# The last two tiles of the out projections, the layer norm and the first two tiles of the next stage, by halves of the 512 tokens

## The chip, the cores and the metric

The kernel runs on one core of one Trainium2 chip. The time is the device time of one execution in microseconds. A core has five engines that run side by side, each through its own instructions in order: PE (matrix multiplication), DVE (vector), ACT (activations and copies), POOL (general vector work) and SP, which here only issues DMAs. They wait for each other by semaphores.

## The reference

Two blocks follow each other on a sequence of 512 tokens with 2048 features, all in float32. The first has two layers of one form:

```python
for l in range(DEPTH):                       # 2 layers
    u = x @ w_in[l]                          # 2048 -> all branches
    y_conv, y_mla, y_rwkv = ...              # convolution, attention, RWKV-7
    mix = jnp.concatenate([y_conv, y_mla, y_rwkv], axis=-1)      # 2048 features
    x = _layer_norm(DEEPNORM_ALPHA * x + mix @ w_out[l], ln_g[l], ln_b[l])
```

The second block begins with `h = rms_norm(x, ln_gain)` and `proj = h @ w_in_2` and goes on with differential attention, a state-space branch, gates, two projections and an output projection, to which x is added. A layer norm needs the mean and the variance over all 2048 features of a token, so nothing of the next stage's `x @ w_in` for a token can start before the whole out projection of that token is done.

## The kernel before

Activations lie transposed: features on the 128 partitions, tokens along the free axis. A vector of 2048 features is 16 tiles of 128 x 512. Float32 products are made of three passes: weights and activations are each split into a rounded high part (fp32r) and a low part, and `mm3` (lines 178 to 185) adds high x high, high x low and low x high, 48 matmuls for one output tile of 128 features. `load_w` brings a tile's weights in two pieces of 512 KB; ACT casts the high part (`wh`, three buffers) and DVE subtracts for the low part (`wl`, three buffers).

The instructions of each engine are put in order when the program is built, by a scheduler that reckons with its own times; on the chip each engine keeps that order. Around the change the order of work is this:

- `out_proj` (line 1100) makes 16 output tiles. Each gets the residual added on DVE (line 1146) and its square from ACT (line 1153). POOL adds tiles and squares up over the tiles (lines 1163, 1164); in the last layer DVE keeps three weighted sums more (lines 1166, 1168), since layer norm and the next block's RMS norm are folded into one step there. Between the tiles, the preparation of the state-space branch (`ssm_prep`) runs in pieces on DVE, ACT and POOL.
- While the last tile is on PE, small matmuls against unit vectors (line 1138) turn the running sums into per-token columns in PSUM (`ps_st`); the last tile's own share comes last (lines 1175, 1177).
- DVE works out mean and variance in columns of four numbers per partition (lines 1186 to 1196), POOL the power of -1/2 (line 1202), twice in the last layer. PE transposes the columns into rows (lines 376, 1238), ACT copies these to SBUF (lines 1239, 1241).
- For each of the 16 tiles a multiply (line 1250, five of them on POOL), a matmul of six rows for the shift (line 1252), a multiply-add that reads it from PSUM (line 1253) and the split into high and low part (lines 175 and 176, three low parts on POOL) make the next stage's x.
- The next stage begins with two output tiles at once (`inproj_group`, line 193): for each feature tile q, as soon as its x is there, six matmuls. The third output tile needs one of the two accumulators and so waits until a copy on ACT has freed it.

This happens twice: between the layers, and between the second layer and the second block. Between two boundaries PE works through tiles of `mm3` one behind the other.

## Time and profile before

| | us |
|---|---|
| median of 3 runs | 3318.41 |
| lowest, highest | 3317.36, 3320.7 |
| profiled execution | 3319.2 |
| its span, first to last instruction | 3317.5 |

| engine | busy us | share of the span | instructions |
|---|---|---|---|
| PE matmul | 3271.4 | 99% | 16291 |
| DVE | 1738.0 | 52% | 2783 |
| ACT | 1123.2 | 34% | 1842 |
| POOL | 706.9 | 21% | 925 |

Matmuls are pipelined: one of 512 columns is shown as busy for 0.39 us, but the next starts 0.23 us later. So a stretch in which PE is shown as busy all the time may still be one in which it runs below its rate: the starts say more than the busy time. Granted clock is the share of TensorE's full clock of 2.4 GHz; the lower of its two levels is 1.2 GHz.

### The profile page before, as it was taken

The numbers are of one execution on the slowest core, as the hardware profiler recorded it, in microseconds if no ns is written. First come the engines' busy times: TensorE is split into PE (matmuls) and PEld (weight loads), VectorE is DVE, ScalarE is ACT, GpSimd is POOL, SyncE is SP. The second block draws the span as 40 slices with busy tenths as digits, with TensorE's granted clock in tenths as the row PEclk, the third lists the DMA queues.
The fourth block names the chain that finished last, engine by engine and source line by source line (L and its number), as shares of the span: only waits on it lengthen the run. The fifth ranks groups of instructions, "written<-read, shape, count | busy, mean of one in ns | idle before, by whom it ended". The sixth has DMA issues, their size and how long they took to land. (4 is left out here: it accounts for less than half of the span.)

```text
span 3317.5 us, 42703 instructions
## 1 busy us (share of the span) xinstructions
PE 3271.4 (99%) x16291; PEld 2686.6 (81%) x16291; DVE 1738.0 (52%) x2783; ACT 1123.2 (34%) x1842; POOL 706.9 (21%) x925
## 2 busy tenths in 40 slices
PE   9999999999999999999999999999999999999999
PEld 7787888877878778888878688888888888888887
DVE  4536835655663459446567666555555533323432
ACT  4332223444333222224532234344444322222332
POOL 1234622012421036321123321111110000001011
PEclk9999999999999999999999899999999999999999
DMA  6455544435544554445255243333333633333543
GB/s 173 149 178 151 145 128 146 125 89 157 168 151 126 151 160 131 144 134 154 80 157 150 84 117 105 102 102 102 100 98 119 221 102 105 102 106 101 158 146 111
DMA packets 672832, 433.81 MB, mean 131 GB/s; under 512 B 91286, under 2 KB 615851, under 8 KB 672627
## 3 DMA queue, kind: packets, MB, share of 16 engines
q1 hardware_dynamic: 668754, 419.02, 42.5%
q0 software_dynamic: 3296, 11.01, 1.1%
q8 instruction: 128, 2.10, 0.3%
q10 hardware_dynamic: 576, 1.05, 0.1%
q14 instruction: 78, 0.63, 0.1%
HBM read 351.30 MB, written 79.69 MB: 130 GB/s over the span
## 5 line engine op out<-in xcount | busy, mean ns | idle before, releaser
L183 PE MATMUL acc<-xh,wh 128*128 128x512 f32 x3552 | 1394.1, 394 | 11.3 <-ACT c L778 5.0
L185 PE MATMUL acc<-xh,wl 128*128 128x512 f32 x3552 | 1398.4, 394 | 2.0 <-DVE wl L169 2.0
L184 PE MATMUL acc<-xl,wh 128*128 128x512 f32 x3552 | 1397.5, 394 | 2.6 <-DVE xl L176 2.3
L169 DVE TENSOR_TENSOR wl<-wr,wh 128x1024 fp32r<-128x1024 f32 (+1 forms) x508 | 662.4, 1304 | 873.5 <-ACT wh L168 850.3
L168 ACT CAST wh<-wr 128x1024 fp32r<-128x1024 f32 (+1 forms) x508 | 530.5, 1045 | 1468.4 <-PE acc L184 1204.0
L183 PEld LDWEIGHTS acc<-xh,wh 128*128 128x128 f32 x3552 | 669.3, 189 | 155.0 <-ACT c L778 6.1
L184 PEld LDWEIGHTS acc<-xl,wh 128*128 128x128 f32 x3552 | 669.1, 188 | 147.7 <-DVE xl L176 6.8
L185 PEld LDWEIGHTS acc<-xh,wl 128*128 128x128 f32 x3552 | 669.2, 188 | 140.5 <-DVE wl L169 2.9
L1836 POOL TENSOR_TENSOR b<-b,b 128x512 f32<-128x512 f32 x16 | 21.1, 1316 | 499.0 <-DVE b L1834 499.0
L396 POOL TENSOR_TENSOR rr_a<-rv_a,mhalf 128x8 f32<-128x8 f32 (+1 forms) x24 | 35.9, 1495 | 280.7 <-DVE rv_a L391 280.7
L1163 POOL TENSOR_TENSOR b<-b,b 128x512 f32<-128x512 f32 x28 | 49.6, 1772 | 181.4 <-DVE b L1146 174.8
L1834 DVE SCALAR_TENSOR_TENSOR b<-b,ps_b 128x512 f32<-128x512 f32 x32 | 22.0, 688 | 105.5 <-PE ps_b L185 105.5
L598 DVE TENSOR_TENSOR pk<-pk,pk 128x224 f32<-128x224 f32 (+59 forms) x126 | 69.9, 555 | 3.4
L599 DVE TENSOR_TENSOR pk<-pk,pk 128x224 f32<-128x224 f32 (+59 forms) x126 | 65.3, 518 | 3.5
L966 POOL TENSOR_TENSOR v<-v,c 128x512 f32<-128x512 f32 x16 | 20.6, 1288 | 185.0 <-ACT v L963 185.0
L562 DVE TENSOR_TENSOR pk<-ps_m,mrk 128x512 f32<-128x512 f32 x32 | 22.0, 689 | 68.9 <-PE ps_m L559 68.8
L825 ACT ACTIVATE a<-ps_a,nm_a,sp_a 128x128 f32<-128x128 f32 (+3 forms) x64 | 39.2, 615 | 44.1 <-DVE nm_a L822 40.4
L1854 POOL TENSOR_TENSOR b<-b,ln 128x512 f32<-128x512 f32 x16 | 20.7, 1293 | 151.6 <-DVE b L1853 126.1
L183 PE MATMUL acc<-n,wh 128*128 128x512 f32 x128 | 52.4, 409 | 0.1
L694 POOL COPY zw_pk<-zwh_pk 64x128 f32<-64x128 f32 x64 | 22.0, 343 | 139.8 <-ACT zwh_pk L687 137.0
L184 PE MATMUL acc<-n,wh 128*128 128x512 f32 x128 | 51.2, 400 | 0.0
L183 PE MATMUL ps_b<-ya,wh 128*128 128x512 f32 x128 | 50.7, 396 | 0.0
(519 smaller groups left out, 4017.2 us busy)
## 6 DMA issues: line engine op xcount, KB each, us to landing
wr<-in_w_in_dram SPq DMA_DIRECT2D x336, 512.0 KB
wr<-in_w_out_dram SPq DMA_DIRECT2D x96, 512.0 KB
pack<-pk SPq DMA_DIRECT2D x32, 576.0 KB
pk<-pack SPq DMA_DIRECT2D x24, 576.0 KB
b<-xd SPq DMA_DIRECT2D x48, 256.0 KB
c<-mix SPq DMA_DIRECT2D x32, 256.0 KB
xd<-b SPq DMA_DIRECT2D x32, 256.0 KB
wr<-in_w_proj_att_dram SPq DMA_DIRECT2D x16, 512.0 KB
```

Source lines behind the costliest of these rows:

```text
L168: nc.scalar.copy(hi[:, : m * n], raw[:, : m * n])
L169: nc.vector.tensor_tensor(out=lo[:, : m * n], in0=raw[:, : m * n], in1=hi.bitcast(F32)[:, : m * n], op=ALU.subtract)
L183: self.nc.tensor.matmul(out, lhsT=wh, rhs=xh, start=st, stop=False)
L184: self.nc.tensor.matmul(out, lhsT=wh, rhs=xl, start=False, stop=False)
L185: self.last = self.nc.tensor.matmul(out, lhsT=wl, rhs=xh, start=False, stop=sp)
L396: nc.gpsimd.tensor_tensor(out=r.rearrange(flat), in0=v.rearrange(flat), in1=k.mhalf[:, 0:n], op=ALU.pow)
L562: nc.vector.tensor_tensor(out=pk[:, i, O_G:].rearrange("p (h c t) -> p h c t", h=2, c=2), in0=ps[:, :, 0:256].rearrange("p h (c t) -> p h ...
L598: eng.tensor_tensor(out=t3, in0=X[:, 0:n, c - 1 : c].to_broadcast([P, n, w]), in1=q[:, q.shape[1] - w :].unsqueeze(1).to_broadcast([P, n, ...
L599: eng.tensor_tensor(out=X[:, 0:n, c:], in0=X[:, 0:n, c:], in1=t3, op=A)
L694: nc.gpsimd.tensor_copy(out=Wd[o, u, c].rearrange("p (h w) -> p h w", w=64), in_=Wh[o, u, 0:4:3, :])
L825: nc.scalar.activation(out=pr[:, 0:n], in_=ps[:, 0:n], func=AF.Exp, scale=scale, bias=nm, accum_out=sm)
L1163: nc.gpsimd.tensor_tensor(out=sums[0], in0=sums[0], in1=t, op=ALU.add)
```

## The change

- The last two of the 16 output tiles, 14 and 15, are made in halves of 256 tokens: both tiles for the first 256, then both for the second, with the weights of both kept. `load_w` gets a parameter `spare`: the second piece of tile 15's weights goes into two buffers of the `r4` kind, which are otherwise the preparation's.
- Tiles 14 and 15 are no longer added to the running sums. Their share of the columns comes by small matmuls, per half and tile.
- The columns, the powers, the transposes and the copies are made per half (`stats(h)`), each with two columns in place of four. The multiply now always reads ACT's copy of the row (`As`), no longer PSUM.
- Normalisation and split go in the order: tiles 0 to 7 of the first half, tiles 0 to 7 of the second, tiles 8 to 15 of the first, and of the second. `inproj_group` follows this order for the stages behind a layer norm. Each output row of x is written to memory in two DMAs.
- PSUM: three `b` and one `st` buffers become two and two.

```diff
-    def load_w(self, parts, kt, n, side=False):
+    def load_w(self, parts, kt, n, side=False, spare=None):
...
+                if spare and k0 + m == kt:
+                    hi, lo = (self.b4((P, WCH), F32R, spare) for _ in range(2))
+                else:
...
-        for q in range(KT):
-            for i, ps in enumerate(pss):
-                self.mm3(ps, sub(w[q : q + 1], slice(i * P, i * P + P)), x[q : q + 1], q == 0, q == KT - 1)
+        for q0 in range(0, KT, KT // 2):
+            for ts in HALVES if halves else (slice(0, S),):
+                for q in range(q0, q0 + KT // 2):
+                    for i, ps in enumerate(pss):
+                        self.mm3(ps[:, ts], sub(w[q : q + 1], slice(i * P, i * P + P)), sub(x[q : q + 1], ts),
+                                 q == 0 and ts.start == 0, q == KT - 1 and ts.stop == S)
...
-    with k.phase(f"p{l}o", {"b": 3, "r": 2, "st": 1}, b=26, r=14, r4=2):
+    with k.phase(f"p{l}o", {"b": 2, "r": 2, "st": 2}, b=29, r=14, r4=2):
...
+    tail = [(c, weights(c, spare="r" if c == KT - 1 else None), residual(c), k.b(), k.b()) for c in (KT - 2, KT - 1)]
+    z += [t for _, _, _, t, _ in tail]
+    for h, ts_ in enumerate(HALVES):
+        pss = [k.ps((P, S // 2), tag="r") if h else k.acc((P, S // 2)) for _ in tail]
+        for ps, (c, wt, xt, t, sq) in zip(pss, tail, strict=True):
+            k.mm3(ps, [wt[q] for q in MIX_ORDER], sub([m2[q] for q in MIX_ORDER], ts_))
...
+            nc.vector.scalar_tensor_tensor(out=t[:, ts_], in0=xt[:, ts_], scalar=ALPHA, in1=ps, op0=ALU.mult, op1=ALU.add)
+            nc.scalar.activation(out=sq[:, ts_], in_=t[:, ts_], func=AF.Square)
+        for c, _, _, t, sq in tail:
+            for i in range(2):
+                o = (2 * h + i) * P
+                nc.tensor.matmul(psts[h][:, i, 0:nz], lhsT=t[:, o : o + P], rhs=wz[:, c, 0:nz], start=False, stop=False)
+            for i in range(2):
+                o = (2 * h + i) * P
+                nc.tensor.matmul(psts[h][:, i, nz:ns], lhsT=sq[:, o : o + P], rhs=wz[:, c, 0 : ns - nz], start=False, stop=(c == KT - 1 and i == 1))
...
+    def stats(h):
+
+        pst = psts[h]
+        mean = ts(pst[:, :, 0:1], 1.0 / D, M)
+        var = stt(pst[:, :, nz : nz + 1], 1.0 / D, tt(mean, mean, M), M, SB)
+        rs = power(ts(var, 0.0, ALU.max, LN_EPS, A))
...
+        for i in range(2):
+            nc.tensor.transpose(pA[:, i], A_[:, i].to_broadcast([P, P]), k.ident)
...
+        for i in range(2):
+            nc.tensor.transpose(p6[:, i], c6[:, i].rearrange("p a b -> p (a b)"), k.ident)
+        nc.scalar.copy(r6, p6.rearrange("p i t -> p (i t)"))
+        nc.scalar.copy(As, pA.rearrange("p i t -> p (i t)"))
+        return As, r6
+
+    parts = [stats(h) for h in range(2)]
...
+    for q0 in range(0, KT, KT // 2):
+        for (As, r6), ts_ in zip(parts, HALVES, strict=True):
+            for q in range(q0, q0 + KT // 2):
+                pool, zq = q in PA, z[q][:, ts_]
+                with k.tc.issue_after(outs[-LAG].ins) if len(outs) >= LAG and not pool else nullcontext():
+                    (nc.gpsimd if pool else nc.vector).tensor_tensor(out=zq, in0=zq, in1=As, op=M)
+                pr, y, o = k.ps((P, S // 2), tag="rb"[q % 2]), k.b((P, S // 2)), slice(32 * (q // 4), 32 * (q // 4) + 6)
+                nc.tensor.matmul(pr, lhsT=gb[o, q % 4], rhs=r6[o], start=True, stop=True)
+                outs.append(nc.vector.scalar_tensor_tensor(out=y, in0=zq, scalar=gl(q), in1=pr, op0=M, op1=A))
...
+                k.lows.append(k.split(y, nx[q][0][:, ts_], nx[q][1][:, ts_], nc.gpsimd if q in PL else None))
```

In the changed kernel the lines move: 1175 and 1177 become 1205 and 1208, 376 and 1238 become 1271 and 1282, 1202 becomes 1236, 1250, 1252 and 1253 become 1298, 1300 and 1301, 176 and 183 to 185 become 180 and 187 to 189, and 1146 for tiles 14 and 15 becomes 1200.

First PE, at the end of the first layer's out projection. Before, from the last matmul of tile 15 on (`acc` with `xh` and `wl`; `ps_st` are the column sums, `ps_b` from `col_b` and from `b` with `ident` the transposes, `acc` with `xh` and `wh` at the end the next stage):

```order
L185 MATMUL acc_8032<-xh_6668,wl_8028 128x512
L1175 MATMUL ps_st_6692<-wz_b_6682,b_8083 128x1 x4
L1177 MATMUL ps_st_6692<-wz_b_6682,b_8085 128x1 x4
L376 MATMUL ps_b_8107<-ident,col_b_8103 128x128 x4
L1238 MATMUL ps_b_8121<-ident,b_8114 128x128 x4
L1252 MATMUL ps_r_8131<-b_8122,b_6933 128x512
L1252 MATMUL ps_b_8142<-b_8122,b_6933 128x512
L1252 MATMUL ps_r_8153<-b_8122,b_6933 128x512
```

The changed kernel in the same place, from the first half's transposes on, which stand behind the last matmul of the second half (`ps_st_6693` belongs to the second half; `b_8219` is the first half's row):

```order
L1271 MATMUL ps_b_8217<-ident,col_b_8213 128x128 x2
L1282 MATMUL ps_b_8231<-ident,c_b_8224 128x128 x2
L1205 MATMUL ps_st_6693<-wz_b_6682,b_7973 128x1 x2
L1300 MATMUL ps_r_8284<-b_8219,b_6934 128x256
L1300 MATMUL ps_r_8304<-b_8219,b_6934 128x256
L1208 MATMUL ps_st_6693<-wz_b_6682,b_7974 128x1 x2
L1271 MATMUL ps_b_8248<-ident,col_b_8244 128x128 x2
L1282 MATMUL ps_b_8262<-ident,c_b_8255 128x128 x2
L1300 MATMUL ps_b_8294<-b_8219,b_6934 128x256
L1300 MATMUL ps_r_8324<-b_8219,b_6934 128x256
L1300 MATMUL ps_b_8314<-b_8219,b_6934 128x256
L187 MATMUL acc_8587<-xh_8288,wh_8592 128x256
```

The second half's last sums and its transposes stand among the first half's L1300 and ahead of the next stage's first matmul.

DVE in the same place. Before, from the columns behind POOL's power to the first multiply-adds:

```order
L1228 SCALAR_TENSOR_TENSOR fb_b_8105<-col_b_8095,col_b_8103 128x4
L1231 CAST fh_b_8113<-fb_b_8105 128x8
L1234 COPY b_8114<-fh_b_8113 128x16x2
L1235 TENSOR_TENSOR b_8114<-fb_b_8105,fh_b_8113 128x16
...
L1250 TENSOR_TENSOR b_6927<-b_6927,ps_b_8107 128x512
L1253 SCALAR_TENSOR_TENSOR b_8132<-b_6756,par_117,ps_r_8131 128x512
L1253 SCALAR_TENSOR_TENSOR b_8143<-b_6823,par_117,ps_b_8142 128x512
```

The changed kernel, from the last of the first half's three early multiplies on (`col_b_8244` is the second half's power, `b_8218` the first half's `As`):

```order
L1298 TENSOR_TENSOR b_6928<-b_6928,b_8218 128x256
L1225 TENSOR_SCALAR col_b_8236<-ps_st_6693 128x2
...
L1225 TENSOR_SCALAR col_b_8242<-col_b_8240 128x2
L1272 SCALAR_TENSOR_TENSOR fb_b_8246<-col_b_8236,col_b_8244 128x2
L1275 CAST fh_b_8254<-fb_b_8246 128x4
...
L1279 TENSOR_TENSOR c_b_8255<-fb_b_8246,fh_b_8254 128x8
L1301 SCALAR_TENSOR_TENSOR b_8285<-b_6757,par_117,ps_r_8284 128x256
L1301 SCALAR_TENSOR_TENSOR b_8295<-b_6824,par_117,ps_b_8294 128x256
L180 TENSOR_TENSOR xl_8289<-b_8285,xh_8288 128x256
```

All columns of the second half, those that need its power too, now stand ahead of the first half's first multiply-add.

POOL there, before (the power and the five multiplies that follow it):

```order
L1202 TENSOR_TENSOR col_b_8103<-col_b_8101,mhalf 128x4
L1250 TENSOR_TENSOR b_7043<-b_7043,b_8128 128x512
L1250 TENSOR_TENSOR b_7361<-b_7361,b_8128 128x512
L1250 TENSOR_TENSOR b_7591<-b_7591,b_8128 128x512
L1250 TENSOR_TENSOR b_7844<-b_7844,b_8128 128x512
L1250 TENSOR_TENSOR b_8083<-b_8083,b_8128 128x512
```

and in the changed kernel:

```order
L1236 TENSOR_TENSOR col_b_8213<-col_b_8211,mhalf 128x2
L1298 TENSOR_TENSOR b_7044<-b_7044,b_8218 128x256
L1298 TENSOR_TENSOR b_7362<-b_7362,b_8218 128x256
L1298 TENSOR_TENSOR b_7592<-b_7592,b_8218 128x256
L1298 TENSOR_TENSOR b_7845<-b_7845,b_8218 128x256
L1298 TENSOR_TENSOR b_7973<-b_7973,b_8218 128x256
L1236 TENSOR_TENSOR col_b_8244<-col_b_8242,mhalf 128x2
L1298 TENSOR_TENSOR b_7044<-b_7044,b_8249 128x256
```

The second half's power stands behind all five multiplies of the first half (four of them in the second layer).

## Rows read from the trace of the kernel before

**Rows 1.** The page: busy us of each engine (share of the span), instructions.

```profile
PE 3271.4 (99%) x16291; PEld 2686.6 (81%) x16291; DVE 1738.0 (52%) x2783; ACT 1123.2 (34%) x1842; POOL 706.9 (21%) x925
```

**Rows 2.** Windows: length, busy us per engine, granted clock, DMA share, GB/s.

```profile
937.30:954.60 17.30, 13.13 (x41) 8.11 (x41) 12.88 (x27) 5.13 (x10) 7.23 (x6) 0.61 0.43 135
1868.00:1893.00 25.00, 17.77 (x51) 11.55 (x52) 19.67 (x48) 7.31 (x12) 10.37 (x11) 0.60 0.15 46
```

**Rows 3.** Timeline, PE, first boundary: start, duration, idle before and its releaser.

```profile
936.16 0.39 PE L185 MATMUL acc<-xh,wl 128*128 128x512 f32 x1
937.33 1.05 PE L1175 MATMUL ps_st<-wz_b,b 128*128 128x1 f32 x8 [0.78 <-DVE b L1146]
...
941.24 1.11 PE L376 MATMUL ps_b<-ident,col_b 128*128 128x128 f32 x4 [1.96 <-POOL col_b L1202]
...
948.35 1.22 PE L183 MATMUL acc<-xh,wh 128*128 128x512 f32 x2
...
979.12 0.50 PE L183 MATMUL acc<-xh,wh 128*128 128x512 f32 x1 [0.81 <-ACT w L418]
```

**Rows 4.** Timeline, PE, second boundary.

```profile
1867.44 0.39 PE L185 MATMUL acc<-xh,wl 128*128 128x512 f32 x1
...
1874.93 1.11 PE L376 MATMUL ps_b<-ident,col_b 128*128 128x128 f32 x4 [4.37 <-DVE col_b L1186]
...
1882.22 1.22 PE L183 MATMUL acc<-xh,wh 128*128 128x512 f32 x2
...
1915.05 0.50 PE L183 MATMUL acc<-xh,wh 128*128 128x512 f32 x1 [0.67 <-ACT s L1577]
```

**Rows 5.** Timeline, DVE, first boundary: columns, multiplies, multiply-adds, last splits.

```profile
941.22 0.17 DVE L1228 SCALAR_TENSOR_TENSOR fb_b<-col_b,col_b 128x4 f32<-128x4 f32 x1 [1.14 <-POOL col_b L1202]
...
941.88 0.18 DVE L1235 TENSOR_TENSOR b<-fb_b,fh_b 128x16 f32<-128x16 f32 x1
944.37 1.88 DVE L1250 TENSOR_TENSOR b<-b,ps_b 128x512 f32<-128x512 f32 x3 [2.31 <-ACT b L1241]
946.17 0.74 DVE L1253 SCALAR_TENSOR_TENSOR b<-b,par,ps_r 128x512 f32<-128x512 f32 x1
946.83 0.74 DVE L1253 SCALAR_TENSOR_TENSOR b<-b,par,ps_b 128x512 f32<-128x512 f32 x1
...
970.34 2.33 DVE L176 TENSOR_TENSOR xl<-b,xh 128x512 fp32r<-128x512 f32 x3
```

**Rows 6.** Timeline, POOL, first boundary.

```profile
940.15 1.03 POOL L1202 TENSOR_TENSOR col_b<-col_b,mhalf 128x4 f32<-128x4 f32 x1 [10.64 <-DVE col_b L1191]
944.42 6.20 POOL L1250 TENSOR_TENSOR b<-b,b 128x512 f32<-128x512 f32 x5 [3.24 <-ACT b L1241]
```

**Rows 7.** Timeline, PE at full clock: 512 columns, 18 apart; 256 columns, three apart.

```profile
925.70 0.39 PE L183 MATMUL acc<-xh,wh 128*128 128x512 f32 x1
...
929.77 0.39 PE L183 MATMUL acc<-xh,wh 128*128 128x512 f32 x1
...
1641.17 0.28 PE L923 MATMUL acc<-wh,n 128*128 128x256 f32 x1
...
1641.53 0.28 PE L923 MATMUL acc<-wh,n 128*128 128x256 f32 x1
```

**Rows 8.** Timeline and groups by form, 256 columns on DVE and ACT.

```profile
1952.54 0.42 DVE L1605 TENSOR_TENSOR s<-s,s 128x256 f32<-128x256 f32 x1
1952.88 0.42 DVE L1606 TENSOR_TENSOR s<-s,s 128x256 f32<-128x256 f32 x1
...
L1735 DVE SCALAR_TENSOR_TENSOR a<-a,rc_a,a 128x256 f32<-128x256 f32 x8 | 3.9, 485 | 0.3
...
L924 ACT COPY q<-acc 128x256 f32<-128x256 f32 x32 | 12.0, 374 | 7.1 <-PE acc L923 6.7
```

**Rows 9.** Timeline, DVE: the preparation's last step; a DMA of 256 KB, us to landing.

```profile
920.24 0.69 DVE L1444 TENSOR_TENSOR r<-r,r 128x512 f32<-128x512 f32 x1
...
pk<-T POOLq DMA_DIRECT2D x12, 256.0 KB, 5.6
```

More of the change, by code (lines that the diff above doesn't have):

```diff
@@ L1125, in out_proj @@
         nc.gpsimd.memset(unit[:, q, q : q + 1], 1.0)
-    zero = k.small((P, 4 * ns), "zero", 1)
+    zero = k.small((P, 2 * ns), "zero", 1)
     nc.gpsimd.memset(zero, 0.0)
@@ L1129, in out_proj, with weights, residual @@
     sums = [k.b() for _ in range(ns)]
-    pst = k.ps((P, 4, ns), tag="st")
+    psts = [k.ps((P, 2, ns), tag="st") for _ in HALVES]
     wo = a["w_out"][l]
-    for c in range(KT):
-        if c == KT - 1:
-            nc.tensor.matmul(pst.rearrange("p i q -> p (i q)"), lhsT=k.ident, rhs=zero, start=True, stop=False)
-            for i in range(4):
-                for q in range(ns):
-                    nc.tensor.matmul(pst[:, i], lhsT=sums[q][:, i * P : i * P + P], rhs=unit[:, q], start=False, stop=False)
-        wt = k.load_w([(wo[:, c * P : c * P + P], 0)], KT, P)
-        ps = k.acc()
-        k.mm3(ps, [wt[q] for q in MIX_ORDER], [m2[q] for q in MIX_ORDER])
+    def weights(c, **kw):
+        return k.load_w([(wo[:, c * P : c * P + P], 0)], KT, P, **kw)
+    def residual(c):
         xt = k.b()
@@ L1144, in out_proj, with keep @@
             nc.sync.dma_start(out=xt, in_=xd[c])
+        return xt
+    def keep(t):
+        d = k.dp.tile([P, S], F32, name=k.nm("xd"))
+        nc.sync.dma_start(out=d, in_=t)
+        nd.append(d)
+    for c in range(KT - 2):
+        wt = weights(c)
+        ps = k.acc()
+        k.mm3(ps, [wt[q] for q in MIX_ORDER], [m2[q] for q in MIX_ORDER])
+        xt = residual(c)
         t = k.b()
@@ L1148, in out_proj @@
         if last:
-            d = k.dp.tile([P, S], F32, name=k.nm("xd"))
-            nc.sync.dma_start(out=d, in_=t)
-            nd.append(d)
+            keep(t)
         sq = sums[nz] if c == 0 else k.b()
         si = nc.scalar.activation(out=sq, in_=t, func=AF.Square)
-        if c == KT - 1:
-            break
         if c == 0:
@@ L1173, in out_proj @@
                 next(k.prep, None)
[L1174 to L1177 removed]
+    tail = [(c, weights(c, spare="r" if c == KT - 1 else None), residual(c), k.b(), k.b()) for c in (KT - 2, KT - 1)]
[4 more added lines that the diff above has]
+            k.mm3(ps, [wt[q] for q in MIX_ORDER], sub([m2[q] for q in MIX_ORDER], ts_))
+            if h == 0 and c == KT - 2:
+                for p, pst in enumerate(psts):
+                    nc.tensor.matmul(pst.rearrange("p i q -> p (i q)"), lhsT=k.ident, rhs=zero, start=True, stop=False)
+                    for i in range(2):
+                        for q in range(ns):
+                            o = (2 * p + i) * P
+                            nc.tensor.matmul(pst[:, i], lhsT=sums[q][:, o : o + P], rhs=unit[:, q], start=False, stop=False)
+            nc.vector.scalar_tensor_tensor(out=t[:, ts_], in0=xt[:, ts_], scalar=ALPHA, in1=ps, op0=ALU.mult, op1=ALU.add)
[7 more added lines that the diff above has]
+                nc.tensor.matmul(psts[h][:, i, nz:ns], lhsT=sq[:, o : o + P], rhs=wz[:, c, 0 : ns - nz], start=False, stop=(c == KT - 1 and i == 1))
+    if last:
+        for _, _, _, t, _ in tail:
+            keep(t)
     n = [0]
@@ L1246, in out_proj @@
+    parts = [stats(h) for h in range(2)]
     nx, outs = [], []
     for q in range(KT):
-        pool = q in PA
-        with k.tc.issue_after(outs[-LAG].ins) if len(outs) >= LAG and not pool else nullcontext():
-            (nc.gpsimd if pool else nc.vector).tensor_tensor(out=z[q], in0=z[q], in1=As if pool else pA, op=M)
-        pr, y, o = k.ps(tag="rb"[q % 2]), k.b(), slice(32 * (q // 4), 32 * (q // 4) + 6)
-        nc.tensor.matmul(pr, lhsT=gb[o, q % 4], rhs=r6[o], start=True, stop=True)
-        outs.append(nc.vector.scalar_tensor_tensor(out=y, in0=z[q], scalar=gl(q), in1=pr, op0=M, op1=A))
```

94 lines of the change are left out of this document (43 added, 51 removed).

## The prediction

> **What bounds the kernel now.** I read the busy shares first, then the windows around the two places where an out projection meets the next stage, then the timelines of PE, DVE and POOL there. The share of busy time says that PE is the bound, 99% busy against 52% for DVE [rows 1], so the only time to win is where PE waits or runs at its lower clock. The windows name the two places: over 17.3 us after the first layer's out projection PE is granted 0.61 of its clock, and over 25 us after the second layer's 0.60 [rows 2]; elsewhere it runs at its upper level of 2.4 GHz. I call them the first and the second boundary, and count time in each from the end of the last out-projection matmul: 936.16 + 0.23 = 936.39, and 1867.44 + 0.23 = 1867.67 [rows 3, 4].
>
> In the first boundary the reader is to see a serial chain. PE waits 0.78 us for the last residual sum, 1.96 us for POOL's power, and starts the next stage's first matmul at 948.35, 11.96 us after zero; the first matmul of that stage's third tile, which is where the disturbance is over, starts at 979.12, 42.7 after zero [rows 3]. In the second it waits 4.37 us for the longer chain of columns, starts the first matmul 14.55 after zero and the third tile 47.4 after zero [rows 4]. Full-speed work in such a stretch is 96 + 16 matmuls of 512 columns, 16 tiny ones and 8 transposes: 112 x 0.226 + 24 x 0.114 = 28.1 us [rows 3, 7]. So 14.6 and 19.3 us are lost, 34 us in all. This is the most that could be won. But from 944.37 to 972.7 DVE works almost without a pause on the normalisation [rows 5]: multiply, multiply-add, low part of the split, 40 instructions of 0.60 or 0.66 us. Behind the visible waits of PE stands a DVE that is full for 28 us.
>
> **Part 1, the tail's matmuls, ahead of zero.** Two tiles of 48 matmuls with 512 columns become 192 with 256. Starts 18 matmuls apart give (929.77 - 925.70) / 18 = 0.226 us for 512 columns; three apart (1641.53 - 1641.17) / 3 = 0.120 us for 256 [rows 7]. So 192 x 0.120 - 96 x 0.226 = +1.3 us per boundary. The column sums of tile 14 no longer go through POOL's running sum but through PE: 8 more matmuls of one to three columns, each of which the trace shows twice, 16 x 0.114 = 1.8 us (eight of them take 1.05 in [rows 3], and 0.25 is the length of one), and a second clearing matmul, 0.2. PE has no gap there: +3.3 us at each boundary, on the path. The DVE and POOL sums that go away lie beside PE and are worth nothing.
>
> TensorE has a price for this in the Trainium skill too ("TensorE: Matmul & The Clock Gate", Back-to-back issue gap): columns at 2.4 GHz plus some 2.5 ns, by which halving would cost 0.2 us per boundary in the tail and not 1.3, and the sum below would be 3317.5. The trace differs, 0.120 against the 0.109 that this gives, and the row is what I use.
>
> **Part 2, the chain after zero, first boundary.** The first half's statistics do get under the second half's matmuls: 34 of these (4.1 us) stand behind its last sum on PE, and POOL's power came 1.9 us after the sums. The second half's do not, and its instructions stand ahead of the first half's in three queues (the order above). Step by step, in us after zero: PE's tiny matmuls 0.9 and four transposes, 1.4; copies of the two rows on ACT, 0.37 each [rows 8] and by estimate 0.3 apart, 2.0 and 2.3; the square behind them on the same engine 2.7; the last sums 3.15; four small columns on DVE 0.8, so 4.1. POOL's power comes after five half multiplies, which started at 2.3 and take half of 6.20 / 5 = 1.24 each [rows 6]: 5.4, and 1.03 more is 6.45. DVE's six columns take 0.85 (941.22 to 942.06) [rows 5]: 7.3. Only now comes DVE's first multiply-add of the first half. Its split waits for ACT, which has the second half's two copies ahead of it (PE's transposes, 7.6, then 0.7), so the next stage's first matmul starts at 8.85, against 11.96 before: a gain of 3.1 us.
>
> **Part 3, DVE after that.** 32 multiply-adds, 19 multiplies (three are done early) and 26 splits of 256 columns. A multiply of 256 columns starts 0.34 after the one before [rows 8], 512 take 0.60; the multiply-add that reads PSUM is 0.66 at 512 [rows 5], and 256 columns at 0.96 GHz less make 0.39. So 32 x 0.39 + 45 x 0.337 = 27.7, two weight splits of 1.15 that fall in between 2.3, and 1.9 of waits (0.7 for the first split, the rest as before, where 28.3 us held 26 of work): 7.3 + 31.9 = 39.2. Then the last five matmuls on PE 0.6 and the wait for the accumulator's copy, 0.8 in the row at 979.12, with its start 1.0: the third tile starts at 40.8, against 42.7. Gain 1.8 or 1.9; I take 1.8. PE itself would need 8.85 + 220 x 0.12 = 35.3 (192 of the two tiles, 28 of L1300). In the gaps from 3 to 8 it falls to its lower clock again; now that lasts (1 - 0.61) x 2 x 17.3 = 13.5 us [rows 2], of which some 8.6 would lie behind 8.85 and cost half, 4.3: 39.6. DVE and PE end close to each other, and neither lets the other gain. With DVE's waits between 0 and 4 us this gain lies between 3.7 and -0.3.
>
> **Part 4, second boundary.** The same with the longer columns. Of the 4.37 us that their chain takes now [rows 4] two powers of 1.03 are POOL's; DVE's 2.3 I split into 0.8 ahead of the first power, 1.2 between and 0.3 behind. The second half's sums end at 3.35; POOL's first power waits for four half multiplies, to 4.95, and ends at 5.97; columns 1.2, second power to 8.2, the last column and the five that follow 1.1: 9.3, and the first matmul 10.85. DVE's 30 us and 1.9 of waits: 41.2, third tile 42.8 against 47.4. Gain 4.6 (between 2 and 6.5).
>
> **Part 5, the borrowed weight buffers.** Tile 15's second half of weights goes into the two buffers that hold the state-space preparation's cosines. In the first boundary the low part must wait until these are written out. The preparation's last DVE step ends at 920.93 [rows 9]; three ACT instructions 2.2, the write between nothing and the 5.6 us of a transfer of that size [rows 9], the split 1.2: 924.3 to 929.9. PE is there at about 927.6 (tile 14 starts at 912.8, then 99 half matmuls and 24 tiny ones). A wait between 0 and 2.3; I take 1.0, between the two ends. In the second boundary there is no preparation left: 0. The residuals' DMAs double to 32 of 128 KB on SP, with weight loads behind them; the third tile's first load passes after 19 of them, 25 us after zero and 15 ahead of its use: 0. The order of the stage after the second boundary also changes, among matmuls that are all ready: 0, give or take 2.
>
> **Sum.** First 3.3 - 1.8 + 1.0 = +2.5; second 3.3 - 4.6 = -1.3; together +1.2. The profiled execution took 3319.2 us, 1.7 more than its span, and so would become 3320.4; it stood 0.8 above the median of the runs, 3318.4, so I predict 3319.6. The bounds of the terms give -3.6 to +7.2, that is 3315 to 3326.
>
> **Rivals.** (a) The halves overlap as they look on paper: the second half's statistics do not hold the first half's multiply-adds, and DVE starts on them when the first half's row is copied, at 2.3 in both. Then 5.0 and 6.9 us more are won: 3307.7. For it: the first half's chain is fully covered. Against: POOL and DVE take their instructions in order, and the rows above put the power behind five multiplies and the columns ahead of the first multiply-add.
> (b) Half instructions on DVE cost their whole busy time, 0.42 for a multiply and 0.49 for a multiply-add [rows 8], not the distance of their starts, since each waits for another engine. 45 x 0.083 + 32 x 0.095 = 6.8 per boundary: 3333.2. For it: the chain DVE, ACT, DVE is in every one of 32 steps; against: the 512-column rows keep 0.60 and 0.66 through the same chain. It decides from 35 ns per instruction on (5.4 us over 154). The Trainium skill has a rule that would do this ("VectorE: DVE Perf Modes", The TRN2 errata: latency is exposed between instructions, so small tiles pay it each time, and 512 elements are advised). By that rule (b) holds; the trace so far disagrees, 0.34 between starts of instructions that are busy 0.42.
> (c) PE keeps its lower clock for 20 us, as in the second boundary now ((1 - 0.60) x 2 x 25) [rows 2]. From some 4 to 24 after zero a matmul then takes 0.22 and not 0.12, 69 are done by 24, the other 151 take 18, and PE ends at 42, some 2 behind DVE: +2 at each boundary, 3323.6.
>
> **Chances.** Forecast with (c) 0.68, (a) 0.16, (b) 0.16. About 0.2%, 6.6 us, is what a measurement of this kernel can tell. (a) is faster by that; a little of the forecast's spread is too; (b) is slower, and so is the forecast's upper end. Faster 0.18, within 0.63, slower 0.19. The range reaches to where half of each rival lies outside: 3309 to 3330.
>
> **What would show it.** Right: the 256-column matmuls 0.120 apart; PE waiting twice after the tail, the longer wait ending with POOL's power behind five L1298; DVE's first L1301 7 and 9 us after zero; third tile 41 and 43 after zero. Wrong: L1301 before the second half's columns, starts of DVE's half instructions over 0.40 apart, a wait over 2 us at the r4 weights, or a loss elsewhere.

## The result, and the profile after

The changed kernel takes 3337.0 us (median of 6 runs, 3335.2 to 3340.5), the kernel before 3318.9 (6 runs). The ratio is 1.0054, with a 95% interval from 1.0044 to 1.0065: slower by 18 us, where 3319.6 was forecast and 3330 was the end of the range. The profiled execution took 3340.5, 3.4 above the median, with a span of 3338.7. By the start of the third tile it has lost 12.9 us at the first boundary (992.00 against 979.12; 1.0 of it arose ahead of the tail, which starts at 913.80 against 912.77) and 21.7 behind the second (1936.71 against 1915.05); after that nothing more.

The page, answering to [rows 1]: the engines' busy time has hardly grown, PE's by the 22 us that have been lost.

```profile
PE 3293.4 (99%) x16743; PEld 2726.5 (82%) x16743; DVE 1750.8 (52%) x2897; ACT 1130.6 (34%) x1882; POOL 703.3 (21%) x946
```

The timeline of PE, first boundary and second, answering to [rows 3, 4]. The last out-projection matmul ends at 941.87 and 1883.14, the new zeros.

```profile
913.80 0.28 PE L187 MATMUL acc<-xh,wh 128*128 128x256 f32 x1
...
948.84 0.69 PE L1271 MATMUL ps_b<-ident,col_b 128*128 128x128 f32 x2 [3.86 <-POOL col_b L1236]
...
951.61 0.80 PE L187 MATMUL acc<-xh,wh 128*128 128x256 f32 x2
...
992.00 0.50 PE L187 MATMUL acc<-xh,wh 128*128 128x512 f32 x1 [1.03 <-ACT w L426]
...
1892.60 0.66 PE L1271 MATMUL ps_b<-ident,col_b 128*128 128x128 f32 x2 [5.97 <-DVE col_b L1220]
...
1895.40 0.80 PE L187 MATMUL acc<-xh,wh 128*128 128x256 f32 x2
...
1936.71 0.50 PE L187 MATMUL acc<-xh,wh 128*128 128x512 f32 x1 [0.88 <-ACT s L1625]
```

The reader is to see that the first in-projection matmul comes 9.74 and 12.26 us after zero (11.96 and 14.55 before), and that the stretch from there to the third tile has grown to 40.4 and 41.3 us (30.8 and 32.8). The gain is where it was forecast; the loss is behind it.

Windows of the changed kernel, answering to [rows 2]: the two stretches at the lower level, the one between the first of them and the third tile, and a piece of the tail.

```profile
946.60:966.70 20.10, 17.25 (x59) 13.23 (x60) 15.13 (x42) 5.81 (x15) 6.95 (x10) 0.50 0.25 86
1888.30:1912.00 23.70, 18.73 (x65) 14.52 (x65) 16.89 (x53) 5.82 (x15) 7.78 (x13) 0.50 0.03 10
966.70:990.00 23.30, 23.14 (x163) 20.34 (x163) 20.73 (x47) 10.21 (x22) 5.70 (x5) 1.00 0.49 153
926.00:929.00 3.00, 3.00 (x16) 3.00 (x15) 1.22 (x1) 0.00 (x0) 0.00 (x0) 0.50 0.14 50
```

The same of the kernel before, cut to where its clock was at the lower level:

```profile
941.00:954.70 13.70, 11.29 (x25) 6.24 (x25) 11.10 (x22) 4.55 (x8) 6.38 (x6) 0.50 0.33 121
1872.90:1893.20 20.30, 16.02 (x36) 9.79 (x37) 16.48 (x35) 6.03 (x10) 9.18 (x9) 0.50 0.01 3
```

PE is at 1.2 GHz for 20.1 and 23.7 us in place of 13.7 and 20.3. Its clock falls later and stays down longer, so that 15.1 and 16.6 us of this lie behind the first in-projection matmul (before 6.3 and 11.0). Once at 2.4 GHz PE is busy for 23.14 of 23.30 us and DVE for 20.73: there PE is the bound, not DVE.

Timeline of DVE at the first boundary, answering to [rows 5], then POOL's, answering to [rows 6], then DVE's waits from 949.5 to 990 (what for: us, times, longest).

```profile
944.03 2.15 DVE L1298 TENSOR_TENSOR b<-b,b 128x256 f32<-128x256 f32 x3 [0.88 <-ACT b L1284]
...
949.53 0.47 DVE L1301 SCALAR_TENSOR_TENSOR b<-b,par,ps_r 128x256 f32<-128x256 f32 x1
951.44 0.48 DVE L1301 SCALAR_TENSOR_TENSOR b<-b,par,ps_b 128x256 f32<-128x256 f32 x1 [1.43 <-PE ps_r L1300]
951.84 0.98 DVE L180 TENSOR_TENSOR xl<-b,xh 128x256 fp32r<-128x256 f32 x1
...
968.00 0.48 DVE L1301 SCALAR_TENSOR_TENSOR b<-b,par,ps_b 128x256 f32<-128x256 f32 x1 [1.98 <-PE ps_b L1300]
...
986.45 1.85 DVE L180 TENSOR_TENSOR xl<-b,xh 128x256 fp32r<-128x256 f32 x4
```

```profile
944.08 4.05 POOL L1298 TENSOR_TENSOR b<-b,b 128x256 f32<-128x256 f32 x5 [4.63 <-ACT b L1284]
948.09 0.69 POOL L1236 TENSOR_TENSOR col_b<-col_b,mhalf 128x2 f32<-128x2 f32 x1
```

```profile
DVE b L1301 <- PE ps_r L1300: 2.6, 2, 1.4
DVE b L1301 <- PE ps_b L1300: 2.4, 2, 2.0
```

Two things are new. DVE waits 5.0 us for affine matmuls (the six-row matmuls for the shift, L1300). For 1.4 us of that they stand behind the second half's transposes and copy, for 3.6 us in PE's queue behind in-projection matmuls, most of these at half speed; before, DVE had no such wait after its first multiply. And the first three multiplies take 0.72 each beside POOL's. Their rows show a changed operand: the scale row (the factor of each token) was `pA` in PSUM (`b<-b,ps_b` in [rows 5]) and is now `As` in SBUF (`b<-b,b`), an edit that my prediction passed over.

### The profile page after: what moved, and what is told of

It reads as the page before. It is cut to its first block, busy times and chain, and to the rows that moved or that the text cites. A ratio compares the mean times of both kernels' runs of the same rounds, so it can differ in the third digit from the quotient of the medians.

```text
span 3338.7 us, 43824 instructions
## 1 busy us (share of the span) xinstructions
PE 3293.4 (99%) x16743; PEld 2726.5 (82%) x16743; DVE 1750.8 (52%) x2897; ACT 1130.6 (34%) x1882; POOL 703.3 (21%) x946
## 4 chain that ended last, share of the span: by engine, by line
PE 51%; DVE 1%; DMA 1%; issue 0%; ACT 0%; SPq 0%; POOL 0%; DVEq 0%; ACTq 0%; POOLq 0%
PE acc L188 13%; PE acc L187 13%; PE acc L189 13%; PE ps_b L188 2%; PE ps_b L187 2%; PE ps_b L189 2%; PE ps_s L944 1%; PE ps_a L1804 0%; PE ps_o L848 0%; PE ps_s L1676 0%; PE ps_s L1681 0%; PE ps_a L374 0%; PE ps_s L1647 0%; DMA c<-mix 0%; PE ps_a L1777 0%
## 5 line engine op out<-in xcount | busy, mean ns | idle before, releaser
L188 PE MATMUL acc<-xl,wh 128*128 128x512 f32 (+1 forms) x3600 | 1401.3, 390 | 1.7 <-DVE xl L180 1.5
L187 PE MATMUL acc<-xh,wh 128*128 128x512 f32 (+1 forms) x3600 | 1391.1, 390 | 10.9 <-ACT c L786 5.0
L189 PE MATMUL acc<-xh,wl 128*128 128x512 f32 (+1 forms) x3600 | 1399.4, 389 | 1.8 <-DVE wl L173 1.8
L188 PEld LDWEIGHTS acc<-xl,wh 128*128 128x128 f32 x3600 | 682.0, 189 | 144.3 <-DVE xl L180 6.4
L187 PEld LDWEIGHTS acc<-xh,wh 128*128 128x128 f32 x3600 | 678.5, 190 | 147.0 <-ACT c L786 6.1
L189 PEld LDWEIGHTS acc<-xh,wl 128*128 128x128 f32 x3600 | 682.3, 190 | 135.5 <-DVE wl L173 3.1
L179 ACT CAST xh<-b 128x256 fp32r<-128x256 f32 (+1 forms) x96 | 44.0, 477 | 39.9 <-DVE b L1301 36.0
```

The costliest lines, as they stand in the source:

```text
L179: self.nc.scalar.copy(hi, src)
L187: self.nc.tensor.matmul(out, lhsT=wh, rhs=xh, start=st, stop=False)
L188: self.nc.tensor.matmul(out, lhsT=wh, rhs=xl, start=False, stop=False)
L189: self.last = self.nc.tensor.matmul(out, lhsT=wl, rhs=xh, start=False, stop=sp)
```

## The experiments

Zero, first in-projection matmul and third tile below are from each run's profiled execution; times are medians, ratios against the kernel before on the same chip. A "fill" is a matmul on ready operands whose result is overwritten or never read.

**1. Keep PE busy in its longest wait.** The changed kernel:

```diff
+        if h:
+            with k.tc.issue_after(end.ins):
+                for _ in range(WARM):
+                    nc.tensor.matmul(pA.rearrange("p i t -> p (i t)"), lhsT=gb[:, 0], rhs=gb[:, 0:2].rearrange("p c n -> p (c n)"), start=True, stop=True)
```

`WARM` is 36, and `end` is the last column sum.

> The changed kernel with 36 more matmuls of 256 columns at each boundary, behind the last column sums and ahead of the second half's transposes; what they write is overwritten by these. They fill PE's wait for the second half's power (3.9 and 6.0 us), after which PE was seen at its lower level of 1.2 GHz for 20.1 and 23.8 us. From the first in-projection matmul to the third tile the changed kernel takes 40.4 and 41.3 us where 31.95 were forecast. Theory C (the clock): PE at half speed for 15.1 and 16.7 us of this stretch is what sets its length. Then the granted clock stays up, the third tile starts some 43 and 46 us after zero (now 50.1 and 53.6), and the kernel takes about 3322. Theory D (DVE): 154 half instructions with their waits fill DVE for 38 us whatever PE's clock is. Then the clock rises and the third tile stays at 50 and 53: 3335 to 3338. Theory S (switches): on PE each change between an affine matmul of 6 rows and an in-projection matmul costs some 0.24 us, 18 to 21 pairs in place of 6 to 8: the clock's share of PE's time goes, the 4 us of switches stay: 3326.

3340.4 us, 1.0066 (1.0049 to 1.0083): no gain. At the first boundary the clock stayed up from zero until 950.9 and was then at its lower level for some 13.7 us. It fell at this wait:

```profile
952.03 0.58 PE L189 MATMUL acc<-xl,wh 128*128 128x256 f32 x1 [2.06 <-DVE xl L181]
```

DVE's first split stood behind two multiplies that took 1.66 us beside POOL (0.75 later on). C's premise was not met, so this does not tell C from D; it pointed to POOL.

**2. The same on the kernel before.** 9 or 19 fills of 512 columns behind the column sums, 4 behind the transposes.

> The kernel before with 13 (first boundary) and 23 (second) more matmuls of 512 columns in PE's waits: 9 and 19 behind the last column sums, 4 behind the transposes; their results are overwritten. There PE was at its lower level for 6.3 and 10.9 us behind the first in-projection matmul. Theory C: what PE loses to the lower level in this stretch is on the path, so half of 17 us comes back: about 3311. Theory D: DVE, full for 28 us from its first multiply on, sets the third tile in the kernel before, and the clock is hidden: 3317 to 3321. Theory S says the same as D here, the switches are few.

3320.0, 1.0006 (0.9996 to 1.0015). The time at the lower level became shorter, 10.2 us at each boundary (13.7 and 20.3 before), but it was moved: all of it now lies behind the first in-projection matmul, where 6.3 and 11.0 us were. The time is D's number, but C's premise was not met here either. The first boundary:

```profile
948.50:958.70 10.20, 9.29 (x20) 6.03 (x21) 10.20 (x17) 3.52 (x6) 3.28 (x3) 0.51 0.41 157
```

**3. The second half's statistics later**, rival (a) made true:

```diff
-    parts = [stats(h) for h in range(2)]
+    parts = [stats(0)]
...
+                if len(outs) == LATE:
+                    parts.append(stats(1))
```

`LATE` is 4, and `outs` counts the multiply-adds.

> The changed kernel with the second half's statistics written behind the first half's first four multiply-adds, so that the second half's columns no longer stand ahead of DVE's first multiply-add, which was 7.7 us after zero (949.5). This is my rival (a) made true. Theory D: DVE starts on the normalisation 5 and 7 us earlier and the third tile with it: 3325. Theory C: PE has in-projection matmuls to do in place of its longest wait, the clock falls later or not at all, and more than that comes back: 3318 or less. Theory S: the earlier start alone, some 4 and 5 us: 3328.

3332.4, 1.0043 (1.0028 to 1.0058). The first in-projection matmul came 5.3 us after zero at both boundaries, 4.5 and 7 earlier, and the third tile still 49.0 and 49.7 after it (50.1, 53.6). At the first boundary PE waited 1.59 us for DVE's first multiply-add and 2.05 us for the second half's first low part, and its clock fell at about these two places. An earlier start by itself is not what the end hangs on.

**4. In-projection over all tokens**: `halves=False` at both calls of `inproj_group`.

> The changed kernel with the next stage's first two tiles over all 512 tokens again (96 matmuls of 512 columns in place of 192 of 256); tail, statistics and normalisation stay in halves. The first in-projection matmul then waits until the first half of eight tiles is done, some 8 us. Theory D: DVE has the same work and the third tile stays where it is: 3334 to 3339. Theory C: PE waits longer, more of its work falls to the lower level: 3340 to 3348. Theory S: fewer matmuls between which to switch and 1.3 us less per boundary: 3332.

3349.5, 1.0095 (1.0080 to 1.0110), beyond C's end: the first in-projection matmul came 18.7 and 21.3 us after zero.

**5. The operand, by itself, in the kernel before.**

```diff
-            (nc.gpsimd if pool else nc.vector).tensor_tensor(out=z[q], in0=z[q], in1=As if pool else pA, op=M)
+            (nc.gpsimd if pool else nc.vector).tensor_tensor(out=z[q], in0=z[q], in1=As, op=M)
```

> The kernel before with one operand changed: DVE's eleven multiplies of the normalisation read the scale row from its SBUF copy, as POOL's five do and as in the changed kernel, and no longer from PSUM. Theory P (POOL beside DVE): a DVE instruction with both operands in SBUF is slowed while POOL multiplies. In the changed kernel three multiplies of 256 columns took 2.15 us beside POOL, 0.72 each, where they start 0.335 apart elsewhere, and two 1.43, while the multiply-adds, which read PSUM, kept 0.39; in the kernel before one split took 1.16 beside POOL where its like start 0.60 apart, and three multiplies that read PSUM kept 0.63. By P the first five multiplies, which lie beside POOL's 6.2 us, lengthen by about 0.5 us each, and the third tile comes some 2 us later at each boundary: 3321 to 3324. Theory L (lock step: DVE and PE wait in turn for each other in twice as many steps): the operand's place is worth nothing: 3317.5 to 3319.5.

3324.8, 1.0017 (1.0007 to 1.0026): 5.6 us slower, as P says. DVE, then POOL; to be held against [rows 5, 6], where the same three took 1.88 and the same five 6.20:

```profile
943.67 4.04 DVE L1250 TENSOR_TENSOR b<-b,b 128x512 f32<-128x512 f32 x3 [2.31 <-ACT b L1241]
...
948.95 1.67 DVE L1250 TENSOR_TENSOR b<-b,b 128x512 f32<-128x512 f32 x1
```

```profile
943.72 8.03 POOL L1250 TENSOR_TENSOR b<-b,b 128x512 f32<-128x512 f32 x5 [3.23 <-ACT b L1241]
```

With both operands in SBUF a DVE multiply takes 1.33 us beside POOL and 0.60 alone, and POOL's are slowed too, 1.6 for 1.24. The Trainium skill has this rule ("SBUF — State Buffer", Who interferes with whom): a DVE instruction with two SBUF inputs contends with a GpSimd (here POOL) instruction that reads SBUF; one with at most one SBUF input, outside DVE's 2-port modes, does not. The traces agree on both halves of it: 1.33 for 0.60 us with two SBUF inputs, and 0.63 for 0.60 with the row in PSUM.

The slower multiplies also make PE wait, 3.15 us at once where it was 0.99, and its lower level then lasts 23.8 us at each boundary (13.7 and 20.3 before). So part of this operand's price is paid through the clock:

```profile
937.50:961.30 23.80, 17.29 (x43) 10.96 (x43) 19.11 (x35) 6.02 (x10) 10.85 (x7) 0.50 0.34 119
1872.80:1896.60 23.80, 16.30 (x37) 9.92 (x38) 19.47 (x37) 6.03 (x10) 11.77 (x11) 0.50 0.05 14
```

**6. No POOL multiplies**: `PA = ()` in the changed kernel.

> The changed kernel with POOL's ten half multiplies given to DVE. Theory P: the slowing goes (about 1.1 us before the second half's columns and 1.9 around the first in-projection matmul), the second half's power no longer stands behind five POOL multiplies (3 us), and ten half multiplies of 0.335 are added; first in-projection matmul some 6 us after zero (now 9.7), third tile about 46 (now 50.1): 3329 to 3332. Theory L: DVE has 3.4 us more to do in the stretch that PE and DVE go through in step, with an earlier start of 3: 3336 to 3340. Theory D (DVE is full): 3.4 us more per boundary, 3344.

3335.5, 1.0048 (1.0032 to 1.0065). The first in-projection matmul came 7.5 and 10.2 us after zero, the third tile 50.1 and 51.5. The earlier start is there, but the stretch behind it did not become shorter (42.6 and 41.3 us). That DVE's ten extra multiplies take what the missing contention gives is a reading of this, not shown by itself. The time is just below L's range.

**7. Normalisation and in-projection by halves, on the kernel before**; tail, statistics and the row in PSUM as they were.

> The kernel before with only the normalisation's multiplies, affine matmuls, multiply-adds and splits and the next stage's first two tiles by halves; the out projection's tail and the statistics stay over all tokens, and DVE reads the scale row from PSUM. Theory L: twice the steps make the stretch from the first in-projection matmul to the third tile some 39 us long, as in the changed kernel (40.4, 41.3; before 30.8, 32.8), and the chain ahead of it keeps its 12 and 14.5 us: third tile 51 and 53 after zero, 3333 to 3336. Theory P: without the operand in SBUF this stretch takes 33 to 34 us: 3321 to 3325. My forecast's own terms (27.7 us of half instructions in place of 26): 3320.

3325.5 (ten runs, 3321.0 to 3326.9), 1.0018 (1.0009 to 1.0028); stretches of 37.9 and 35.3 us. Between L and P, nearer to P: the halves cost something with the row in PSUM, but not 18.

**8. Runs 3 and 6 together** (statistics late, `PA = ()`).

> The second half's statistics behind the first four multiply-adds, as in the run before of that name (3332.4), and POOL's ten half multiplies given to DVE. There PE still waited 2.2 us for the first low part, behind three DVE multiplies slowed by POOL, and 2.0 us at the second half's first one; its clock fell at both. Theory P: both waits go and PE's clock stays up for most of the stretch: 3321 to 3326. Theory L: 3332 with 3.4 more on DVE per boundary, less some 2 for the waits: 3333 to 3337.

3330.8, 1.0034 (1.0021 to 1.0047): neither. PE still waited 0.8 and 0.6 us for splits and its clock fell.

**9. More fills in the kernel before.** Run 2, and behind affine matmuls:

```diff
+        if q in FILL:
+            scr = scr or k.ps(tag="st")
+            warm(FILL[q], scr, aff)
```

`FILL` asks for 8 fills behind the fourth affine matmul and 6 behind the eighth; `scr` is the bank of the statistics, free by then.

> The kernel before with PE's waits filled further: beside the fills of the earlier run on this kernel (9 or 19, and 4, matmuls of 512 columns), 8 more behind the fourth affine matmul and 6 behind the eighth, into a free PSUM bank, where PE waited 1.8 and 1.4 us and its clock fell. In the kernel before PE is at its lower level for 6.3 and 10.9 us behind the first in-projection matmul; from 954.7 on it has no pause, and DVE's last split ends at 972.7, 6.4 us ahead of the third tile. Theory C (PE's clock sets the stretch): with the clock up to the end, half of 6.3 and 10.9 us comes back: 3310 to 3312. Theory D (DVE's 28 us set it, as my prediction says): 3317 to 3320.

3313.9, 0.9990 (0.9981 to 0.9999), 4.6 us faster: the only version that beats both kernels, by little. At the second boundary the clock stayed up and the third tile came 43.6 us after zero (47.4 before):

```profile
1872.00:1913.00 41.00, 39.97 (x163) 28.04 (x162) 32.57 (x68) 14.89 (x22) 17.92 (x20) 1.00 0.22 66
```

At the first boundary of the same execution (3318.0 us, 4 above the median) the clock fell all the same, for 6.8 and 3.4 us, and the third tile came 45.4 us after zero (42.7 before).

So in the kernel before, too, PE's clock was on the path, as the second boundary shows. D, on which my third part rests, does not hold there; by the medians alone its range (3317 to 3320) and the interval just touch.

**10. More fills in the changed kernel.** Run 1, and 17 fills behind the seventh affine matmul.

> The changed kernel with the 36 fills in the wait for the second half's power, and 17 more matmuls of 256 columns behind the seventh affine matmul, where PE then waited 2.1 us for the first low part and its clock fell. Theory C: the clock stays at its upper level over the stretch, DVE's waits for affine matmuls queued on PE behind slow in-projection matmuls (5.1 us in the changed kernel) go, and the third tile starts some 44 us after zero (now 50.1): 3324 to 3328. Theory D and theory P (POOL beside DVE): DVE's work and what POOL adds to it set the stretch: 3335 to 3339.

3330.2, 1.0043 (1.0030 to 1.0057). From ahead of the first in-projection matmul on the clock stayed up at both boundaries. The stretches shrank to 36.5 and 36.4 us, and the third tile came 47.0 us after zero at the first boundary, half of the way to the 44 that C promised:

```profile
946.00:985.00 39.00, 38.46 (x260) 32.81 (x258) 34.25 (x86) 16.40 (x38) 10.67 (x11) 1.00 0.41 136
```

**11. The operand put back in the changed kernel**: the two rows in the banks of the statistics, `in1=As if pool else pA`.

> The changed kernel with one thing undone: DVE's multiplies read the scale row from PSUM again, as in the kernel before (the two rows take the banks of the two statistics, which are free by then). In the run that put the row into SBUF in the kernel before, three multiplies took 4.04 us beside POOL (1.88 before) and POOL's five 8.03 (6.20), and the kernel became 5.6 us slower. Theory P: as much comes back here, DVE's three first multiplies take 1.0 us (now 2.15) and POOL's five some 3.1 (now 4.05), so that the second half's power is 1 us earlier too: 3329 to 3333. Theory L: no change, 3336 to 3338.

3330.0, 1.0036 (1.0022 to 1.0049): 7 us come back, as P says. The lower level lasts 10.1 and 13.5 us here, in place of 20.1 and 23.7. DVE's three and POOL's five now:

```profile
945.06 1.08 DVE L1298 TENSOR_TENSOR b<-b,ps_st 128x256 f32<-128x256 f32 x3 [0.88 <-ACT b L1284]
```

```profile
945.10 3.46 POOL L1298 TENSOR_TENSOR b<-b,b 128x256 f32<-128x256 f32 x5 [4.63 <-ACT b L1284]
```

**12. Runs 3 and 11 together.**

> The second half's statistics behind the first four multiply-adds (3332.4 alone) and the scale rows read from PSUM. Theory P: another 5 us come back: 3326 to 3329. Theory L: 3331 to 3334. If both waits at the first low parts go and PE's clock stays up (C), 3322 or less.

3325.5, 1.0026 (1.0015 to 1.0036), just below P's range; still above the kernel before.

**13. Runs 10 and 11 together.**

> The changed kernel with both: scale rows read from PSUM (3330.0 alone), and PE's two waits filled with 36 and 17 matmuls (3330.2 alone; the 17 go into one of the banks of the affine matmuls here). If operand and clock are two causes that add up, 7.1 and 6.8 us come back together: 3322 to 3325. If they are one cause seen twice (the slowed DVE makes PE wait, and that lets the clock fall), the second adds nothing: 3328 to 3331.

3332.9, 1.0043 (1.0028 to 1.0058), spoilt by its own fills: they waited for the statistics' bank and ran until 3.5 us behind the power (949.8), the first part of them at half speed (granted clock 0.73 from 947.4 to 953.4).

```profile
947.43 5.96 PE L1274 MATMUL ps_st<-b 128*128 128x256 f32 x36 [0.87 <-DVE col_b L1231]
```

**14. Only tail and statistics by halves**; normalisation and in-projection over all tokens, one row in PSUM.

> The changed kernel with the normalisation and the next stage's first two tiles over all tokens again, as in the kernel before; the tail and the statistics stay in halves, and DVE reads one row for all tokens from PSUM. What the tail costs by itself: from the traces, tiles 14 and 15 with their sums took 4.4 and 2.7 us longer than before (3.3 each forecast), and the chain behind them starts the in-projection some 1 us earlier at the first boundary and 1 to 2 at the second. Tail alone: 3322 to 3325. With the normalisation by halves alone at plus 6 to 7 and the operand at plus 5.6 to 7 the three then make up the 18. If the shorter chain pays for the tail, 3317 to 3320.

3331.5, 1.0038 (1.0023 to 1.0052): 13 us slower, where the tail (4.4 and 2.7) less the earlier start of the in-projection (2.1 and 2.6) makes 2.4. The clock stayed at its lower level for 27.5 and 30.4 us, most of it with PE busy:

```profile
946.50:974.00 27.50, 26.05 (x53) 15.48 (x54) 22.86 (x39) 8.29 (x14) 10.18 (x8) 0.50 0.37 133
1882.00:1912.40 30.40, 26.09 (x53) 15.58 (x54) 25.14 (x54) 8.92 (x15) 11.66 (x12) 0.50 0.08 24
```

**15. Run 13 mended**: 24 or 38, and 8, fills in banks that nobody holds.

> The changed kernel with the scale rows in PSUM (3330.0 alone), and PE's waits filled with 24 (first boundary) or 38 and then 8 matmuls of 256 columns into banks that nobody holds. In the run before of this kind the fills waited 0.9 to 2.7 us for the bank of the statistics, ended 1.5 to 2 us behind the power and ran at the lower clock, so that it said nothing of the sum. Two causes that add: first in-projection matmul some 9.5 and 12 us after zero, third tile 44 and 46: 3322 to 3326. One cause seen twice: 3328 to 3331.

3328.0, 1.0024 (1.0013 to 1.0035). The profiled execution has the third tile at 44.9 and 45.9, as two causes would; the median has 2 us less than either repair alone. They overlap for the most part.

**16. Run 14 with fills** (18 or 34 ahead of the second transposes, then as run 9).

> The kernel with only tail and statistics in halves (3331.5), and PE's waits filled: 18 or 34 matmuls of 256 columns ahead of the second half's transposes, 8 of 512 behind the fourth and 6 behind the eighth affine matmul. There PE's clock was at its lower level for 28 and 30 us from the wait for the second half's power on (13.7 and 20.2 in the kernel before), 22 of them behind the first in-projection matmul. Theory C: with the clock up the stretch from there to the third tile takes 31 to 33 us and not 38.1 and 38.6: 3318 to 3322, the tail's own cost less what the chain gains. If the halves cost by themselves: 3328 to 3332.

3318.9, 0.9999 (0.9990 to 1.0009): 12.6 of the 13 us are back. At the second boundary the third tile came 41.8 us after zero, and the stretch took 29.3 us with the clock up, fills included, where the same work took 38.6 in run 14. At the first one the clock fell at about 941 all the same, and the third tile came 48.5 after zero; this execution, 3321.7 us, was the longest of the ten.

```profile
1884.00:1917.00 33.00, 32.45 (x126) 22.50 (x126) 29.21 (x44) 13.90 (x22) 15.38 (x15) 1.00 0.21 65
940.90:962.00 21.10, 20.32 (x57) 14.36 (x57) 16.17 (x33) 5.96 (x11) 8.43 (x7) 0.51 0.34 124
```

The steps from one kernel to the other, in us, as the kernels are and with PE's waits filled:

| in halves | as it is | with fills |
|---|---|---|
| nothing (the kernel before) | 3318.4 | 3313.9 |
| tail and statistics | 3331.5 | 3318.9 |
| and normalisation and in-projection, row in PSUM | 3330.0 | 3328.0 |
| and the row in SBUF (the changed kernel) | 3337.0 | 3330.2 |

The fills differ from version to version, and in the traces of runs 9 and 16 the clock still fell at the first boundary. So the right column is not the time with the clock up throughout.

## Why the prediction was wrong

**What held.** The tail: from 913.80 to 941.87 are 28.1 us; in the kernel before the last 96 matmuls start at 912.77, 23.6 us ahead of zero. That is 4.4 more, and 4.3 were forecast (2.7 for 3.3 at the second boundary); but the r4 wait in it (1.0 forecast) was nil, and in its place 16 matmuls ran at half speed (926 to 929), 1.5 us: the 4.3 came out by luck. The prediction's first paragraph has PE at its upper level everywhere outside the two windows, which misread the kernel before: in its second tail PE was at the lower level for 6.8 us, from the middle of a run of column sums on. The changed kernel has as much there. The kernel before:

```profile
1859.20:1866.00 6.80, 6.80 (x22) 5.81 (x22) 1.13 (x1) 1.04 (x1) 0.00 (x0) 0.50 0.01 2
```

The chain of part 2 held as well: DVE's first multiply-add 7.7 us after zero (7.3 forecast), POOL's power behind five multiplies, first in-projection matmul at 9.7 (8.85). Of part 4: 12.3 (10.85). The spacing 0.120, DVE's 0.39 and 0.335 away from POOL, and the order behind the second boundary, nil. Rival (b) is out by these spacings. Each half instruction does pay a fixed part (2 x 0.335 - 0.60 = 0.07 us for a multiply), but the forecast's spacings held that already; (b)'s further 0.08 and 0.095 did not come.

**The step that failed** is part 3 (and 4 with it): a DVE that is full from its first multiply-add on, 27.7 us of half instructions, 2.3 of weight splits and 1.9 of waits, ends at 39.2 and lets the third tile start at 40.8. DVE ended 46.4 us after zero (988.30), the third tile came at 50.1, and at 53.6 for 42.8. From 949.53 to 988.30 are 38.8 us for 31.9: idle 5.1 for 1.9, and eight instructions beside POOL took 2.8 more than their spacing; the last 0.9 I cannot place. I had taken a DVE full for 28 us as the bound and let PE's clock count for half of 8.6 us. Three things were wrong in that:

- PE's lower level is on the path. Rival (c) had its length right (20 us; 20.1 and 23.7 measured) and its price wrong (2 us per boundary): it counted PE's own delay, and not that DVE's multiply-adds wait in turn for affine matmuls queued on PE. Filling PE's waits is worth 4.6 us in the kernel before, 13 with the tail in halves, 7 in the changed kernel: of the tail's 13 us the longer time at the lower level is the most.
- DVE's operand went from PSUM to SBUF. I cost the multiplies by rows that stood free of POOL; the timeline before had a row that showed the price, a split with two SBUF operands that starts inside POOL's five multiplies (the same split starts 0.60 after the one before it elsewhere):

```profile
950.00 1.16 DVE L176 TENSOR_TENSOR xl<-b,xh 128x512 fp32r<-128x512 f32 x1
```

 Undone it gives 7 us, made alone it costs 5.6. As runs 5 and 11 show, the time at the lower level moves with it, so this is not a sum apart from the first point; run 15 has the overlap.
- PE has more to do than 220 x 0.12. Each change from in-projection to affine matmul and back costs some 0.38 us beyond the four matmuls, at full clock and with DVE long done (theory S of run 1 had 0.24):

```profile
968.70 0.40 PE L187 MATMUL acc<-xh,wh 128*128 128x256 f32 x2
969.03 0.38 PE L1300 MATMUL ps_r<-b,b 6*128 6x256 f32 x1
969.34 0.38 PE L188 MATMUL acc<-xl,wh 128*128 128x256 f32 x1
969.56 0.28 PE L189 MATMUL acc<-xh,wl 128*128 128x256 f32 x1
```

 968.70 to 969.56 is 0.86 for 4 x 0.12. There are 15 such changes behind the first in-projection matmul (18 at the second boundary), 6 in the kernel before: 9 x 0.38 = 3.4, and 1.3 for 192 matmuls in place of 96, is 4.7 at the first boundary (5.9 at the second). With fills the step to halves in normalisation and in-projection costs 9 us (3318.9 to 3328.0), about as much as these make; without fills it is hidden behind the clock (3331.5 to 3330.0). The traces bear the sum out at the second boundary of runs 9 and 15, where from the first in-projection matmul to the third tile the clock is up and PE, the wait for the accumulator's copy apart, has at most 0.2 us of waits:

```profile
1883.55:1913.20 29.65, 28.81 (x113) 20.17 (x112) 25.68 (x39) 12.94 (x20) 11.70 (x13) 1.00 0.24 72
1884.78:1918.80 34.02, 33.08 (x226) 28.49 (x226) 32.24 (x76) 15.60 (x36) 12.24 (x18) 1.00 0.17 48
```

 Less their fills (6 x 0.227 and 8 x 0.120) the two stretches take 28.4 and 33.2 us, 4.8 apart; with 16 changes for 6 the sum gives 5.1 there. The sum was made after the runs, and no run has changed the number of changes alone.

**Rival (a)** came true in run 3 by its own condition and gave 4.6 us, not 12: the earlier start went into later waits. What stays open is what keeps PE at the lower level: why it lasts 13.7 us at one boundary and 27.5 at the same one with only the tail changed, while PE was busy for most of both.

## What to carry to other kernels

Where two engines hand work to and fro in short steps, an earlier start can be worth little if the waits that are left let TensorE's clock fall (run 3: 4.6 us for starts 4.5 and 7 us earlier); look at where the granted clock falls and what work lies behind it before counting a wait as won. Hold every operand of a moved or split instruction against the old one: here PSUM or SBUF decided what it cost beside POOL. And an engine without a pause in one stretch is not yet the bound of it: see which engine is still busy when that one has ended (DVE ended 6.4 us ahead of the third tile in the kernel before).

## What the runs showed of the hardware beyond that

The clock does not fall at the same instruction each time. The kernels of runs 2 and 9 are the same up to here; in one the nine fills ran in 2.35 us, in the other they took 4.19, the clock falling during the column sums ahead of them with no wait in between (run 2, then run 9):

```profile
938.15 1.03 PE L1177 MATMUL ps_st<-wz_b,b 128*128 128x1 f32 x8
939.05 2.35 PE L1183 MATMUL ps_b<-b 128*128 128x512 f32 x9
```

```profile
938.82 1.36 PE L1178 MATMUL ps_st<-wz_b,b 128*128 128x1 f32 x8
940.04 4.19 PE L1184 MATMUL ps_b<-b 128*128 128x512 f32 x9
```

It also fell inside the tail, where PE was busy for 3.00 of 3.00 us (window 926 to 929), behind a run of matmuls with one or two columns; and in the second tail of the kernel before (6.80 of 6.80 us), in the course of 42 matmuls with five columns. The times of the kernel before spread with the mean granted clock: they reach from 3313.5 to 3322.5 us, with 3313.5 to 3314.0 at a clock of 0.994 and 3319.1 to 3322.5 at 0.991.
